# Softmax weights transposed by DMA, as two planes of two-byte words, instead of by TensorE

## The chip, the cores and the metric

The kernel runs on one core of a Trainium2 chip. The core has a matrix engine (TensorE, PE in the profile, with its weight loads as PEld), a vector engine (DVE), a scalar engine (ACT), GpSimd (POOL) and a queue engine that issues DMAs (SP). Each engine works through its own list of instructions in order; semaphores make one wait for another. The metric is the device time of one execution in microseconds (us), and less is better. Three runs of the kernel before took 2072.4, 2073.06 and 2074.07 us.

## The reference

Two transformer layers over 256 tokens of width 2048, all in float32. Each layer is a norm, an attention with 16 heads of 128, a residual, a norm, an MLP with squared ReLU (hidden 8192) and a residual; a last norm ends it. Layer 0 has 8 heads of neighbourhood attention and 8 of dilated attention, layer 1 has 16 heads over 4 shared key/value heads, with a sink logit per head. What matters here is the end of one head, cut down from the reference:

```python
s = jnp.einsum('nkgqd,nksd->nkgqs', qb, kb).astype(jnp.float32) * scale + bias
e = jnp.exp(s - m[..., None])
o = jnp.einsum('nkgqs,nksd->nkgqd', (e / den[..., None]).astype(v.dtype), vb)
```

The normalised weights `e / den` come out with queries along the partitions. The last product needs them with keys along the partitions, so each head's 256x256 weights are transposed once.

## The kernel before

Every large float32 operand is split into a high part that PE takes in its fast float32 form and a low rest (`split`, L92 to L94: ACT writes the high part, DVE the rest), and products of parts are summed. The weight matrices are streamed from DRAM in halves of 512 KB: `fetch` (L105) issues a load into a buffer `r` (six of them) on SP, ACT splits off `h` and DVE `l` (five buffers each), and PE uses them. `fetch` runs three halves ahead in the program; how far SP runs ahead on the chip is set by the `r` buffers.

A projection of one head is a `unit`: two halves, 16 matmuls with the low part (L154) and 16 with the high part (L156). Values for four heads, the output projection and the second MLP product go by `chunk` (L196), with the activations as the stationary operand. All of that is one stream of matmuls on PE. The attention of the heads is laid between these matmuls by a clock that the kernel keeps while it is built: `tick` advances it after each eight matmuls of a unit (four ticks a unit), and `later` puts a piece of work at a number of ticks ahead. Pieces marked narrow go only between the first halves of a unit unless they are four ticks late.

One head (`attend`) has three such pieces, with the distances in `LAGS_0`, `LAGS_1` and `LAGS_END`. `scores` (L341) multiplies q and k, adds the bias and takes the row minimum on DVE (L346), takes exponentials on ACT (L352), adds the sink in layer 1 (L350, L355, L356), and scales by the reciprocal sum on DVE (L359). `weights` (L362) transposes the weights on PE, four 128x128 blocks by a matmul against the identity (L366) into one PSUM buffer `p_ps`, and splits them into `pt`. `values` (L385) multiplies `pt` by the values `v`, and the result is split into `o`.

Layer 0 handles two heads at a time (four units a pair, and a value chunk at every other pair). Layer 1 has one unit of q per head, in two groups of eight heads with two units of k ahead of each. Its last heads' pieces fall into the output projection that follows. The queue of SP holds the weight loads of the whole program, a few loads at the start and the stores at the end, and nothing else. After the pieces are written down a scheduler settles the final order on each engine, moving work of the other engines around it; the order shown further down is the final one.

Of the kernel before, what the change touches and what calls it, by code (L numbers as in the profile page):

```python
# [7 lines left out]
F32 = mybir.dt.float32  # L8
# [6 lines left out]
P = 128  # L15
T = 256
# [14 lines left out]
RAW_BUFS = 6  # L31
PART_BUFS = 5

LAGS_0 = (5,4,3)
LAGS_1 = (4,5,3)
LAGS_END = (3,3,2)


def slopes(n):
# [4 lines left out]
def encoder(ctx: ExitStack, tc: tile.TileContext, a: dict, out: bass.AP):  # L44
    nc = tc.nc
# [7 lines left out]
    aux_ps = ctx.enter_context(tc.tile_pool(name="aux_ps", bufs=1, space=PSUM))  # L53
# [8 lines left out]
    ident = const.tile([P, P], F32, name="ident")  # L62
# [29 lines left out]
    def split(hi, lo, src):  # L92
        nc.scalar.activation(hi, src, AF.Copy)  # L93
        nc.vector.tensor_sub(lo, src, hi.bitcast(F32))  # L94
# [31 lines left out]
    def later(steps, fn, narrow=False):  # L126

        tasks.append((now[0] + steps, len(tasks), fn, narrow))
        tasks.sort(key=lambda t: t[0])
# [195 lines left out]
    def attend(pool, o, head, q, k, v, side, biases, lags, sunk=False):  # L325

        def scores():
            if not q or not k:

                state["late"] = True  # L330
                later(1, scores, True)
                return
            if state.pop("late", False):
                later(2 + 2 * (head % 2), scores, True)
                return
            qh, kh, bias = q[0], k[0], biases()
            s_ps = aux_ps.tile([P, 2, T], F32, name="s_ps", bufs=2)
            for i in range(2):
                qs = slice(i * P, (i + 1) * P)
                for n, (x, y) in enumerate(((0, 0), (0, 1), (1, 0))):  # L340
                    nc.tensor.matmul(s_ps[:, i, :], qh[:, x, qs], kh[:, y, :], start=n == 0, stop=n == 2)  # L341
            s = pool.tile([P, 2, T], F32, name="s", bufs=2)
            st = pool.tile([P, 8], F32, name="st", bufs=4)
            rd = pool.tile([P, 2], F32, name="rd", bufs=4)
            for i in range(2):
                nc.vector.tensor_tensor_reduce(s[:, i, :], s_ps[:, i, :], bias[i], -1.0, 3e38,  # L346
                                               ALU.add, ALU.min, st[:, i:i + 1])
            nm, den = st[:, 0:2], st[:, 2:4]
            if sunk:
                nc.vector.tensor_scalar(nm, nm, sink_neg[:, head:head + 1], None, op0=ALU.min)  # L350
            for i in range(2):
                nc.scalar.activation(s[:, i, :], s[:, i, :], AF.Exp, bias=st[:, i:i + 1], scale=-1.0,  # L352
                                     accum_out=st[:, 2 + i:3 + i])
            if sunk:
                nc.scalar.activation(st[:, 6:8], nm, AF.Exp, bias=sink[:, head:head + 1])  # L355
                nc.vector.tensor_add(den, den, st[:, 6:8])  # L356
            nc.vector.reciprocal(rd, den)
            for i in range(2):
                nc.vector.tensor_scalar(s[:, i, :], s[:, i, :], rd[:, i:i + 1], None, op0=ALU.mult)  # L359
            later(lags[1], lambda: weights(s), True)  # L360

        def weights(s):  # L362
            p_ps = aux_ps.tile([P, 2, T], F32, name="p_ps", bufs=1)
            for j in range(2):
                for i in range(2):
                    nc.tensor.transpose(p_ps[:, j, i * P:(i + 1) * P], s[:, i, j * P:(j + 1) * P], ident)  # L366
            pt = pool.tile([P, 2, 2, T], F32R, name="pt", bufs=2)
            split(pt[:, 0], pt[:, 1], p_ps)
            state["pt"] = pt
            state["at"] = now[0]  # L370
            try_values()

        def try_values():
            if not v or now[0] < state["at"] + lags[2]:
                later(1, try_values, True)
            else:
                values()

        def values():
            pt, vv = state["pt"], v[0]  # L380
            o_ps = aux_ps.tile([P, 512], F32, name="m_ps", bufs=2)
            n = 0
            for j in range(2):
                for x, y in ((0, 0), (0, 1), (1, 0)):
                    nc.tensor.matmul(o_ps[:, :T], vv[:, x, j, side * P:(side + 1) * P], pt[:, y, j, :],  # L385
                                     start=n == 0, stop=n == 5)
                    n += 1
            split(o[0][:, head, 0, :], o[0][:, head, 1, :], o_ps[:, :T])
            heads_done.add(head)

        state = {}
        later(lags[0], scores, True)
# [3 lines left out]
    def project_out(o, which):  # L396
        def done(c, ps, js):
            cs = slice(c * NC, (c + 1) * NC)
            for j in range(2):
                nc.vector.tensor_add(xs[:, j, cs], xs[:, j, cs], ps[j])  # L400
            to_features(c, which)
            for j in range(2):
                squares(c, j)

        def before():
            assert heads_done >= set(range(KT - 2))
            finish_tasks()
            assert heads_done == set(range(KT))

        for c in range(CHUNKS):  # L410
            chunk(o, KT, c, done, before if c == 0 else None)
            if c == 2:
                warm(AF.Sqrt, ssq[:, 0, 0:1])
        heads_done.clear()

    def toeplitz(pool, slope, which):
        def fn():

            if which == 1:
                t = pool.tile([P, 6, GRID], F32, name="rel", bufs=4).rearrange("p j c -> p (j c)")  # L420
            else:
                t = pool.tile([P, TW], F32, name="toep", bufs=2)
            nc.vector.scalar_tensor_tensor(t, tabs[:, 0, :], -slope, tabs[:, which, :],
                                           op0=ALU.mult, op1=ALU.add)
            return [t[:, P - P * i:P - P * i + T] for i in range(2)]
        return fn
# [147 lines left out]
    with tc.tile_pool(name="attn0", bufs=1) as pool:  # L574
# [14 lines left out]
        def grid_bias(h):  # L589
            def fn():  # L590
                rel = rels[h]
                return [rel[:, 2 - 2 * i:6 - 2 * i, :].rearrange("p j c -> p (j c)") for i in range(2)]
            return fn
# [29 lines left out]
        for p in range(8):  # L623
# [3 lines left out]
            for i in range(2):  # L627
                for j, (dst, name, sc) in enumerate(((q, "q", SCALE), (k, "k", 1.0))):
# [3 lines left out]
                    else:  # L632
                        unit(done)
                h = 2 * p + i
                attend(pool, o, h, q[i], k[i], v, h % 4,
                       grid_bias(h) if h < 8 else toeplitz(pool, sl[h - 8], 1), LAGS_0 if p < 7 else LAGS_END)
            if p < 3:
# [10 lines left out]
    with tc.tile_pool(name="attn1", bufs=1) as pool:  # L648
        o = [pool.tile([P, NH, 2, T], F32R, name="o")]
        sl = slopes(16)  # L650
        for p in range(2):
# [11 lines left out]
            for i in range(8):  # L663
# [3 lines left out]
                attend(pool, o, h, q, k[i // 4], v, h // 4, toeplitz(pool, sl[h], 2),  # L667
                       LAGS_1 if h < NH - 3 else LAGS_END, True)
        project_out(o[0], 3)
# [72 lines left out]
```

## Time and profile before

The profiled execution took 2072.76 us, of which 2071.0 us are the span from its first to its last instruction.

| | |
|---|---|
| median of 3 runs | 2073.06 us |
| profiled execution | 2072.76 us |
| span | 2071.0 us |
| granted clock of PE | 0.999 |
| DMA, mean | 187 GB/s |
| transposes on PE (L366) | 128, 19.4 us busy |
| values (L385) | 192, 27.7 us busy |
| scores (L341) | 192, 28.4 us busy |
| weight splits on ACT (L93, `h`) | 716, 757.6 us busy |
| weight splits on DVE (L94, `l`) | 716, 877.9 us busy |

The page gives busy time and its share of the span for each engine, then the chain of work that ended last: it is followed back from the last instruction, at each step to what released that instruction or to the one before it on the same engine. Matmuls are pipelined, so the busy time of a group (128 transposes of 273 ns, of which parts overlap) is more than the place that it takes in the chain; the chain in order of time gives the place. A row of a group of instructions has line, engine, operation, what it writes and reads, the count, then busy time and mean duration, then the engine's idle time just before.

### The profile page before, as it was taken

How to read it: one execution, taken by the hardware profiler on the slowest of the kernel's cores; microseconds unless marked ns; L12 is line 12 of the kernel's file. 1: busy time of each engine (PE TensorE's matmuls, PEld its weight loads, DVE VectorE, ACT ScalarE, POOL GpSimd, SP SyncE). 2: the span in 40 equal slices, each digit the busy share in tenths (PEclk: the TensorE clock that was granted, in tenths of full speed). 3: DMA queues.
4: the chain of work that ended last, by engine and by line, in shares of the span. 5: the costliest groups of instructions: out<-in, count | busy, mean ns of one | idle time of the engine just before them, and what ended most of it. 6: DMA issues, size and time to landing. Idle time of an engine off the chain costs nothing.

```text
span 2071.0 us, 27923 instructions
## 1 busy us (share of the span) xinstructions
PE 2059.9 (99%) x10714; PEld 1770.1 (85%) x10714; DVE 1267.7 (61%) x1790; ACT 1018.2 (49%) x1452; POOL 29.8 (1%) x43
## 2 busy tenths in 40 slices
PE   9999999999999999999999999999999999999998
PEld 8888888888888888888888998888888888888886
DVE  8767765666654456665546887566654446665454
ACT  7555555544533345454445666555443334554443
POOL 2200000000000000000000000000000000000000
PEclk9999999999999999999999999999999999999999
DMA  8755555555666655556655444565556665556663
GB/s 296 232 174 164 172 173 180 185 186 193 190 191 194 194 192 186 191 188 191 192 187 190 162 146 152 183 210 187 189 190 194 193 194 191 191 184 193 193 194 111
DMA packets 108164, 388.28 MB, mean 187 GB/s; under 512 B 12240, under 2 KB 13280, under 8 KB 107648
## 3 DMA queue, kind: packets, MB, share of 16 engines
q1 hardware_dynamic: 106128, 380.46, 57.1%
q0 software_dynamic: 1184, 4.74, 0.8%
q8 instruction: 84, 1.38, 0.3%
q10 hardware_dynamic: 720, 1.31, 0.2%
q14 instruction: 48, 0.39, 0.1%
HBM read 384.36 MB, written 2.10 MB: 187 GB/s over the span
## 4 chain that ended last, share of the span: by engine, by line
PE 98%; DVE 1%; ACT 0%; issue 0%; DVEq 0%
PE acc L156 31%; PE acc L196 26%; PE s_ps L196 21%; PE acc L154 16%; PE s_ps L341 1%; PE m_ps L385 1%; PE p_ps L366 1%; PE m_ps L241 1%; DVE l L94 0%; PE m_ps L518 0%; ACT h L93 0%; ACT gx L560 0%; PE p_ps L156 0%; PE s_ps L156 0%; DVE gx L562 0%
## 5 line engine op out<-in xcount | busy, mean ns | idle before, releaser
L94 DVE TENSOR_TENSOR l<-r,h 128x1024 fp32r<-128x1024 f32 (+1 forms) x724 | 883.5, 1220 | 477.7 <-ACT h L93 465.6
L93 ACT ACTIVATE h<-r 128x1024 fp32r<-128x1024 f32 (+1 forms) x724 | 762.6, 1054 | 538.3 <-PE acc L196 274.1
L156 PE MATMUL acc<-u,h 128*128 128x512 f32 x2848 | 685.8, 391 | 0.0
L156 PEld LDWEIGHTS acc<-u,h 128*128 128x128 f32 x2848 | 522.0, 188 | 99.9 <-ACT h L93 0.2
L154 PEld LDWEIGHTS acc<-u,l 128*128 128x128 f32 x2848 | 366.0, 191 | 12.5
L154 PE MATMUL acc<-u,l 128*128 128x256 f32 x2848 | 376.3, 283 | 0.0
L196 PE MATMUL s_ps<-h,hid 128*128 128x512 f32 x1024 | 317.0, 389 | 0.0
L196 PE MATMUL acc<-h,hid 128*128 128x512 f32 x1024 | 316.7, 389 | 0.0
L217 ACT ACTIVATE t<-acc 128x256 f32<-128x256 f32 x178 | 68.1, 383 | 428.3 <-PE acc L156 428.0
L219 DVE TENSOR_TENSOR z<-acc,t 128x256 f32<-128x256 f32 x178 | 75.7, 425 | 281.9 <-ACT t L217 281.9
L196 PEld LDWEIGHTS s_ps<-h,hid 128*128 128x128 f32 x1024 | 192.3, 188 | 39.7
L196 PEld LDWEIGHTS acc<-h,hid 128*128 128x128 f32 x1024 | 192.3, 188 | 39.7
L196 PE MATMUL s_ps<-l,hid 128*128 128x512 f32 x512 | 199.2, 389 | 0.0
L196 PE MATMUL acc<-l,hid 128*128 128x512 f32 x512 | 199.2, 389 | 0.0
L196 PEld LDWEIGHTS acc<-l,hid 128*128 128x128 f32 x512 | 96.1, 188 | 20.1
L196 PEld LDWEIGHTS s_ps<-l,hid 128*128 128x128 f32 x512 | 96.1, 188 | 19.9
L196 PE MATMUL acc<-h,u 128*128 128x512 f32 x288 | 94.9, 394 | 0.0
L196 PE MATMUL acc<-h,o 128*128 128x512 f32 x256 | 82.1, 392 | 0.0
L196 PE MATMUL s_ps<-h,o 128*128 128x512 f32 x256 | 80.6, 391 | 0.0
L196 PEld LDWEIGHTS acc<-h,u 128*128 128x128 f32 x288 | 54.1, 188 | 10.9
L439 DVE SCALAR_TENSOR_TENSOR z<-z 128x256 f32<-128x256 f32 x128 | 54.4, 425 | 4.3
L196 PEld LDWEIGHTS s_ps<-h,o 128*128 128x128 f32 x256 | 48.1, 188 | 9.9
(130 smaller groups left out, 1081.1 us busy)
## 6 DMA issues: line engine op xcount, KB each, us to landing
r<-in_w_mlp_in SPq DMA_DIRECT2D x256, 512.0 KB, 4.0
r<-in_w_mlp_out SPq DMA_DIRECT2D x256, 512.0 KB, 3.6
r<-in_even_w_in SPq DMA_DIRECT2D x56, 512.0 KB, 3.8
r<-in_odd_w_qkv SPq DMA_DIRECT2D x40, 512.0 KB, 3.8
r<-in_even_w_v SPq DMA_DIRECT2D x32, 512.0 KB, 4.3
r<-in_even_w_out SPq DMA_DIRECT2D x32, 512.0 KB, 3.5
r<-in_odd_w_out SPq DMA_DIRECT2D x32, 512.0 KB, 3.6
r<-in_odd_w_v SPq DMA_DIRECT2D x8, 512.0 KB, 3.5
```

The costliest lines, as they stand in the source:

```text
L93: nc.scalar.activation(hi, src, AF.Copy)
L94: nc.vector.tensor_sub(lo, src, hi.bitcast(F32))
L154: nc.tensor.matmul(ps[:, :T], l, u[:, k[n], 0, :], start=False, stop=stop)
L156: nc.tensor.matmul(ps, h, u[:, k[n]].rearrange("p a t -> p (a t)"), start=k[n] == 0, stop=stop)
L196: nc.tensor.matmul(ps[j], act[:, k, x, tokens], y, start=k == 0 and n == 0, stop=k == nk - 1 and n == 2)
L217: nc.scalar.activation(t, ps[:, T:], AF.Copy)
L219: nc.vector.tensor_add(z, ps[:, :T], t)
L241: nc.tensor.transpose(ps[k // 2][:, k % 2, j * P:(j + 1) * P], xs[:, j, (k0 + k) * P:(k0 + k + 1) * P], ident)
L341: nc.tensor.matmul(s_ps[:, i, :], qh[:, x, qs], kh[:, y, :], start=n == 0, stop=n == 2)
L366: nc.tensor.transpose(p_ps[:, j, i * P:(i + 1) * P], s[:, i, j * P:(j + 1) * P], ident)
L385: nc.tensor.matmul(o_ps[:, :T], vv[:, x, j, side * P:(side + 1) * P], pt[:, y, j, :], start=n == 0, stop=n == 5)
L439: nc.vector.scalar_tensor_tensor(z, z, 0.0, z, op0=ALU.max, op1=ALU.mult)
```

## The change

The four transposes on PE go. In their place `weights` treats each float32 weight as two 16-bit words. Two ACT copies (L369) gather the low words and the high words of all weights into two planes (`planes`). Each plane is transposed as four 128x128 blocks of two-byte words by transposing DMAs on SP (L372), eight a head, into `turned`. A new piece, `join`, set at a fourth distance after `weights`, writes the words back into place: ACT the low words (L379) and DVE the high words (L380) of `pw`, which is then split into `pt` as `p_ps` was. `planes`, `turned` and `pw` have one buffer each. The distances in ticks are changed too.

```diff
-LAGS_0 = (5,4,3)
-LAGS_1 = (4,5,3)
-LAGS_END = (3,3,2)
+LAGS_0 = (5,4,2,5)
+LAGS_1 = (4,4,2,5)
+LAGS_END = (3,3,1,4)
...
         def weights(s):
-            p_ps = aux_ps.tile([P, 2, T], F32, name="p_ps", bufs=1)
-            for j in range(2):
-                for i in range(2):
-                    nc.tensor.transpose(p_ps[:, j, i * P:(i + 1) * P], s[:, i, j * P:(j + 1) * P], ident)
+
+            half = mybir.dt.uint16
+            words = s.rearrange("p i t -> p (i t)").bitcast(half).rearrange("p (i t w) -> p w i t", i=2, w=2)
+            planes = pool.tile([P, 2, 2, T], half, name="planes", bufs=1)
+            turned = pool.tile([P, 2, 2, T], half, name="turned", bufs=1)
+            for w in range(2):
+                nc.scalar.copy(planes[:, w], words[:, w])
+                for j in range(2):
+                    for i in range(2):
+                        nc.sync.dma_start(turned[:, w, j, i * P:(i + 1) * P], planes[:, w, i, j * P:(j + 1) * P],
+                                          transpose=True)
+            later(lags[3], lambda: join(turned), True)
+
+        def join(turned):
+            p = pool.tile([P, 2, T], F32, name="pw", bufs=1)
+            words = p.rearrange("p j t -> p (j t)").bitcast(mybir.dt.uint16).rearrange("p (j t w) -> p w j t", j=2, w=2)
+            nc.scalar.copy(words[:, 0], turned[:, 0])
+            nc.vector.tensor_copy(words[:, 1], turned[:, 1])
             pt = pool.tile([P, 2, 2, T], F32R, name="pt", bufs=2)
-            split(pt[:, 0], pt[:, 1], p_ps)
+            split(pt[:, 0], pt[:, 1], p)
```

In the new file lines after `weights` have moved by 14: values are L399. On SP, in layer 1 after the loads of the first units, before (with -) and now (with +), the transposes stand in line with the weight loads `r`:

```order
 L109 DMA r<-in_odd_w_v 128x1024 x8
-L109 DMA r<-in_odd_w_qkv 128x1024 x36
-L109 DMA r<-in_odd_w_out 128x1024 x32
+L109 DMA r<-in_odd_w_qkv 128x1024 x16
+L372 DMA_TRANSPOSE turned<-planes 128x128 x8
+L109 DMA r<-in_odd_w_qkv 128x1024 x2
+L372 DMA_TRANSPOSE turned<-planes 128x128 x8
+L109 DMA r<-in_odd_w_qkv 128x1024 x2
+L372 DMA_TRANSPOSE turned<-planes 128x128 x4
+L109 DMA r<-in_odd_w_qkv 128x1024
+L372 DMA_TRANSPOSE turned<-planes 128x128 x4
```

Between two heads' eight transposes stand two loads, the two halves of one unit. On ACT, in the same layer, one head before took these rows (`t` and `h` belong to the stream of projections, `s` is the exponential, `o` the result of an earlier head):

```order
L93 ACTIVATE pt<-p_ps 128x512
L352 ACTIVATE s,st<-s,st 128x256 x2
L355 ACTIVATE st<-st,sink 128x2
L217 ACTIVATE t<-acc 128x256
L93 ACTIVATE h<-r 128x1024
L93 ACTIVATE q<-z 128x256
L93 ACTIVATE h<-r 128x1024
L93 ACTIVATE o<-m_ps 128x256
```

Now, from one head's `pw` to the next head's `planes`:

```order
L379 COPY pw<-turned 128x512
L352 ACTIVATE s,st<-s,st 128x256 x2
L355 ACTIVATE st<-st,sink 128x2
L217 ACTIVATE t<-acc 128x256
L93 ACTIVATE pt<-pw 128x512
L93 ACTIVATE h<-r 128x1024
L93 ACTIVATE q<-z 128x256
L93 ACTIVATE o<-m_ps 128x256
L369 COPY planes<-s 128x512 x2
L93 ACTIVATE h<-r 128x1024
```

The next head's `planes` stand behind this head's `pw` and `pt`, and three copies have been added. On PE, in the middle of layer 1's first group of heads, before (-) and now (+), where L385 and L399 are the values:

```order
-L154 MATMUL acc<-u,l 128x256 x8
-L366 MATMUL p_ps<-ident,s 128x128 x4
-L154 MATMUL acc<-u,l 128x256 x8
-L156 MATMUL acc<-u,h 128x512 x16
-L385 MATMUL m_ps<-pt,v 128x256 x6
+L154 MATMUL acc<-u,l 128x256 x16
+L156 MATMUL acc<-u,h 128x512 x16
+L399 MATMUL m_ps<-pt,v 128x256 x6
 L341 MATMUL s_ps<-k,q 128x256 x6
```

The transposes are gone from the stream. The values of a head now stand three units behind its scores, where they stood two behind before: the first values of layer 1 come after the third head's scores.

## The prediction

> **What bounds the kernel now.** I read the page's first part, then the chain that ended last, then that chain in order of time where the softmax weights are transposed, and last what ACT and DVE have left there.
>
> ```profile
> span 2071.0 us, 27923 instructions
> PE 2059.9 (99%) x10714; PEld 1770.1 (85%) x10714; DVE 1267.7 (61%) x1790; ACT 1018.2 (49%) x1452; POOL 29.8 (1%) x43
> PE 98%; DVE 1%; ACT 0%; issue 0%; DVEq 0%
> ```
>
> PE is the bound: it is never idle and it is 98% of the chain. So each matmul taken off it is worth its place in the chain, as long as nothing new makes PE wait. The chain in order of time, in layer 1's attention (start, length, piece):
>
> ```profile
> 1177.14 0.71 PE m_ps L385 x6
> 1177.86 0.72 PE s_ps L341 x6
> 1178.58 0.96 PE acc L154 x8
> 1179.54 0.44 PE p_ps L366 x4
> 1179.97 0.96 PE acc L154 x8
> 1180.93 3.65 PE acc L156 x16
> 1184.59 0.71 PE m_ps L385 x6
> ```
>
> One head takes 7.44 us from values to values (1177.14 to 1184.59): a unit (0.96 + 0.96 + 3.65 = 5.57), scores 0.71, values 0.71 and the four transposes 0.44. The table of stages, over exactly two such heads, shows what is left on the other engines (columns: stage, its length, then busy time of PE, PEld, DVE, ACT, POOL):
>
> ```profile
> 1187.51:1202.39 14.88, 14.88 (x99) 13.59 (x98) 13.52 (x35) 9.87 (x22) 0.00 (x0) 1.00 0.43 141
> ```
>
> Per head DVE works 6.76 of 7.44 us and ACT 4.94. The slack is on ACT; DVE has 0.7 us.
>
> **Removed.** 32 heads x 0.44 us = 14.1 us of PE. A layer-1 head then needs 5.57 + 0.71 + 0.71 = 7.0 us of PE. The old reader of `p_ps`, the split into `pt`, stays and reads `pw`.
>
> **Added, per head.** Two ACT copies into `planes`, eight transposing DMAs on SP, one ACT copy and one DVE copy into `pw`. The nearest rows, 128 partitions by 512 elements:
>
> ```profile
> L93 ACT ACTIVATE pt<-p_ps 128x512 fp32r<-128x512 f32 x32 | 19.0, 592 | 17.9 <-PE p_ps L366 17.7
> L94 DVE TENSOR_TENSOR pt<-p_ps,pt 128x512 fp32r<-128x512 f32 x32 | 21.9, 685 | 0.2
> ```
>
> I take 0.59 us for a copy on ACT and 0.69 on DVE; half of each, and a fifth more, bound them, which moves the sum by a few us. ACT then has 4.94 + 3 x 0.59 = 6.7 us of work in 7.0, DVE 6.76 + 0.69 = 7.45 in 7.0. Already without any wait DVE is over by 0.45 us a head.
>
> The trace of before has no transposing DMA. The rows nearest to it are the plain ones: the issue of a weight load on SP, the dearest issue (POOL's `rev`), and the landing of `rev`, which at 54.8 KB is nearest in size to 32 KB.
>
> ```profile
> L109 SPq DMA_DIRECT2D r<-in_odd_w_qkv x40: 327/328/328, 1077.3 to 1223.0; - x40
> L605 POOL DMA_DIRECT2D rev<-in_rpb x16: 522/526/591, 29.9 to 83.4; - x16
> DMA to landing us min/median/max: 2.4/3.6/13.2
> ```
>
> Call T the time from the first issue of a head's eight to the last landing. Low: 7 x 0.33 + 2.4 = 4.7 us. Chosen: 7 x 0.53 + 3.6 = 7.3 us, since a transposing DMA is no simpler than the dearest plain one and lands among weight loads, as the median of `rev` did. High: each lands before the next begins, 8 x 2.4 = 19.2 us. Below 4.7 it would have to land sooner than any DMA of this trace; that is a rival.
>
> SP issues the transposes in line with the weight loads, so a waiting transpose holds up the loads behind it. That is covered: a load is issued six `r` buffers ahead, with two halves a head 6 x 3.5 = 21 us before its split, and lands in 3.8 us, so 17 us are spare:
>
> ```profile
> r<-in_odd_w_qkv SPq DMA_DIRECT2D x40, 512.0 KB, 3.8
> ```
>
> A price for the issue is stated by the Trainium skill, "VectorE: DVE Perf Modes", section "The three transpose paths": 1309 ns for one 128x128 two-byte transpose by DMA, against 390 by TensorE. No run here shows the first; for the second the chain has 0.44 / 4 = 0.11 us. With 1.309 as issue time, an estimate from that page, T = 7 x 1.309 + 3.6 = 12.8 and the sum below comes to about +200 us, 2270. Against that, the Trainium skill, "Advanced Engine Details and Errata", section "X-Bar Transpose (TRN2)", says that such transposes are as fast as regular DMAs. By it the issue is the 0.33 us of the weight loads, T = 5.9, and the same sum gives +36 us, 2109. Neither is shown by a run here.
>
> **What the transposes collide with.** `planes`, `turned` and `pw` have one buffer each. The eight transposes of head h+1 cannot start before both copies of head h into `pw` are done, and ACT and DVE run in order. From the last landing of h to the first issue of h+1 stand, by the order of ACT: the DVE copy 0.69 (the `pt` split waits for it), `pt` 0.59, an `h` split 1.05, `planes` 0.59, and in half of the heads also `q` and `o`. Rows for these:
>
> ```profile
> 1190.59 1.05 ACT L93 ACTIVATE h<-r 128x1024 fp32r<-128x1024 f32 x1
> 1191.71 0.42 ACT L93 ACTIVATE q<-z 128x256 fp32r<-128x256 f32 x1
> 1193.03 0.36 ACT L93 ACTIVATE o<-m_ps 128x256 fp32r<-128x256 f32 x1
> ```
>
> 0.69 + 0.59 + 1.05 + 0.59 + 0.39 = 3.3 us (0.39 is half of `q` and `o`). So layer 1 has a cycle C = T + 3.3 = 10.6 us a head, against 7.0 of PE. **The wait that takes the place of the transposes is PE's L399, values, on the DVE half of `pt`.**
>
> How much of it is hidden? From the first score of a head to its scaled weights:
>
> ```profile
> 1185.13 0.88 PE L341 MATMUL s_ps<-k,q 128*128 128x256 f32 x6
> 1190.13 0.62 DVE L359 TENSOR_SCALAR s<-s,rd 128x256 f32<-128x256 f32 x2
> ```
>
> 5.62 us (1190.75 - 1185.13). Then `h` 1.05, `planes` 0.59, T, the DVE copy 0.69, `pt` 0.59 + 0.69: 9.2 + T = 16.5 us. In the new order the first values stand three units and three score blocks behind their scores, 3 x (5.57 + 0.71) = 18.8 us: a margin of 2.3.
>
> Layer 1 comes in two groups of eight heads. Between the values of the first and the last head of group one, PE has 7 units, 7 value and 5 score blocks, 47.5 us; it waits 7 x 10.6 - 47.5 - 2.3 = 24.4 us. In group two the last values lie inside the output projection: 2 2/3 units, 7 value and 5 score blocks and 66 matmuls of 0.227 (43.52 / 192, from the chain's row below), 38.5 us; it waits 74.2 - 38.5 - 2.3 = 33.4 us. Layer 1: 57.8 us.
>
> ```profile
> 616.55 43.52 PE s_ps L196 x192
> ```
>
> Layer 0 has 16 heads in 279 us, 17 us each, so the cycle doesn't bind. The stages, layer 1's attention first:
>
> ```profile
> 1145.00:1280.00 135.00, 135.00 (x841) 121.53 (x840) 114.30 (x279) 84.28 (x183) 0.00 (x0) 1.00 0.46 149
> 31.00:310.00 279.00, 278.00 (x1550) 241.75 (x1550) 199.05 (x354) 152.98 (x256) 21.06 (x29) 1.00 0.58 186
> ```
>  But at three of the value chunks (pairs 2, 4 and 6) ACT has only `planes`, `h` and `pw` (2.23 us) between the issue and a `pt` that waits for all eight transposes, and the chunk's `v` copies, on which values wait, are queued behind: 3 x (7.3 + 0.69 - 2.23) = 17.3 us. By PE's new order, at the chain's paces, the last two heads have 13.4 and 12.4 us from scores to values for a chain that without the sink (0.6 us less) takes 15.9: 3.5 us, the first wait carrying over to the second. Layer 0: 20.8 us. Its other heads have some 18 us and are covered; if T passes 9 they are not.
>
> **Sum.** -14.1 + 57.8 + 20.8 = +64.5 us on the profiled execution's 2072.76 us (span 2071.0 and 1.8 around it): 2137 us. The median of the three runs, 2073.06, is 0.3 above that execution, which is nothing here.
>
> **The rivals.** (A) The forecast's mechanism with T between 4.7 and 9: at 4.7, C = 8.0, waits 3.6 + 12.6 + 9.4 + 0.9, sum +12, 2085; at 9, C = 12.3, waits 38.0 + 47.0 + 22.3 + 5.2, sum +98, 2171. Chance 50%.
>
> (B) Dear transposes: one instruction is worked off as a chain of small moves, or each waits for the one before, T from 9 to 19.2. At 12: C = 15.3, the margin is gone (-2.4), waits 62.0 + 71.0 in layer 1, 31.4 + 8.3 and up to 8 x 2.3 for heads no longer covered in layer 0, sum +177, 2250. At 19.2 it is +378, 2451, and the 17 us that cover the weight loads are gone too. For it: eight dependent landings lie on one queue. Against: plain DMAs of one queue overlap. The twelve first loads were issued within 11 us, each 0.4 us long, and landed 4.4 us after their issue:
>
> ```profile
> L530 SPq DMA_DIRECT2D gx<-in_gx x12: 328/427/635, 0.7 to 11.4; - x12
> DMA to landing us min/median/max: 3.3/4.4/7.1
> ```
>
> Chance 34%.
>
> (C) Faster: a copy inside the chip lands sooner than any load here. At T = 4.0 C is 7.3, the waits are 7 in group two and 7.3 at the chunks, and the sum is zero; that is the point from which it decides. At T = 3 only 4.4 us are left at the chunks, the sum is -10 us, and DVE, 0.45 us over per head, takes some of it through later `l` splits: about 2065 us. For it: the trace has only DMAs that read or write DRAM, so nothing shows the landing of this one. Against: eight issues alone take 2.6 us at the cheapest. Chance 10%.
>
> (D) No change: T between the two, 3.7 to 4.3, gains and waits cancel; 2073 us. Chance 6%. That the transposes aren't made is excluded by the order, which has 256 of them and no L366.
>
> **How the numbers follow.** The predicted time is that of A at its chosen T, 2137 us. A and D lie between 2069 and 2171. B adds the upper side; I stop at 2330 (T near 15), which leaves out about 8 in 100 above, and at 2069 below, which leaves out C. About 0.2% (4 us) is what a measurement of this kernel can tell from no change. Faster 10%, within it 6%, slower 84%.
>
> **What would show it.** Right: rows of L372 with an issue of some 0.5 us and 3 to 4 us to landing; PE idle before L399, released by DVE `pt`, some 50 to 60 us in layer 1; ACT idle before `pw`, released by a DMA on `turned`; layer 1's attention, 135 us long before (1145 to 1280), at some 185; no L366. The MLPs unchanged. The size is wrong if T per head isn't 7 us; the mechanism is wrong if PE waits for weight splits instead (SP starved), or if heads of layer 1 follow at 7.5 us with ACT and DVE always busy (C).

## The result and the profile after

The change takes 2292.23 us (median of four, 2289.92 to 2293.43) against 2073.22 for the kernel before on the same chip: a ratio of 1.105 with an interval of 1.104 to 1.107, 219 us slower. The prediction had the sign and the kind of wait, and less than a third of the size. The page of the changed kernel (span, busy time by engine, the granted clock in 40 slices of 57 us, the chain by engine):

```profile
span 2290.1 us, 28206 instructions
...
PE 2115.5 (92%) x10586; PEld 1802.8 (79%) x10586; DVE 1270.1 (55%) x1822; ACT 1066.1 (47%) x1548; POOL 26.7 (1%) x43
...
PEclk9989898999999999999999878799999999999999
...
PE 75%; SPq 11%; DVE 5%; DMA 4%; ACT 3%; issue 1%; DVEq 0%; ACTq 0%
```

PE was idle for 11.1 us of the span before (2071.0 - 2059.9) and is for 174.6 now: 163.5 more. Its busy time should have fallen by the 14.1 us of the transposes, to 2045.8, and is 69.7 above that. 163.5 + 69.7 - 14.1 = 219.1 us, the whole loss. The clock digits fall where the two attentions lie, and nowhere else.

Where each layer loses is read from the start of the first 43.52 us block of each MLP, in the chain in order of time; before:

```profile
573.03 43.52 PE acc L196 x192
...
1535.70 43.52 PE acc L196 x192
```

and after:

```profile
676.84 43.52 PE acc L196 x192
...
1755.36 43.52 PE acc L196 x192
```

Layer 0's attention has become 103.8 us longer, layer 1's 115.9 (219.7 - 103.8); the MLPs take what they took. What the transposes cost on SP (minimum, median and maximum in ns, then the landing) and who stands for them (total us, times, longest), from the view of one line and from the view of waits:

```profile
L372 SPq DMA_TRANSPOSE turned<-planes x256: 1093/1230/2527, 49.7 to 1493.6; - x128
...
DMA to landing us min/median/max: 2.2/2.4/10.3
```

```profile
DVE pw L380 <- DMA turned<-planes: 250.8, 32, 9.2
ACT pw L379 <- DMA turned<-planes: 114.1, 27, 8.6
...
PE m_ps L399 <- ACT pt L93: 69.8, 17, 6.7
...
PE m_ps L399 <- ACT v L319: 31.8, 3, 10.6
...
PE acc L196 <- DVE z L219: 18.9, 4, 6.6
```

SP stands 1.23 us at each transposing DMA, not 0.53, and one lands 2.4 us after its issue begins, not 3.6. The chain through one head of layer 1 shows the eight one after the other (start, length, piece):

```profile
1258.98 0.52 ACT planes L369
...
1259.56 1.11 SPq L372
...
1260.72 1.22 SPq L372
...
1268.36 2.41 DMA turned<-planes
...
1270.90 0.47 DVE pw L380
...
1273.60 1.13 ACT planes L369 x2
```

From 1259.5 to the last landing at 1270.8 are T = 11.3 us, and from one head's `planes` to the next 14.6 us (1273.60 - 1258.98), against 7.0 of PE's work. Over the seven steps of each group of eight heads the mean from first issue to first issue is 14.4 and 14.3 us. In layer 1's attention PE is busy for two thirds, at a clock of 0.81, and in layer 0's for 81%, at 0.90 (same columns as the stages before):

```profile
31.00:414.00 383.00, 308.54 (x1525) 260.53 (x1523) 203.61 (x371) 177.56 (x305) 20.48 (x28) 0.90 0.48 147
1249.00:1500.00 251.00, 165.59 (x784) 140.72 (x783) 116.39 (x296) 109.80 (x232) 0.00 (x0) 0.81 0.33 99
```

### The profile page after: what moved, and what is told of

The parts are those of the page before. It is cut to its first block, busy times and chain, and to the rows that moved or that the text cites. A ratio compares the mean times of both kernels' runs of the same rounds, so it can differ in the third digit from the quotient of the medians.

```text
span 2290.1 us, 28206 instructions
## 1 busy us (share of the span) xinstructions
PE 2115.5 (92%) x10586; PEld 1802.8 (79%) x10586; DVE 1270.1 (55%) x1822; ACT 1066.1 (47%) x1548; POOL 26.7 (1%) x43
## 4 chain that ended last, share of the span: by engine, by line
PE 75%; SPq 11%; DVE 5%; DMA 4%; ACT 3%; issue 1%; DVEq 0%; ACTq 0%
PE acc L156 23%; PE s_ps L196 19%; PE acc L196 19%; PE acc L154 12%; SPq L372 11%; DMA turned<-planes 3%; DVE l L94 2%; ACT planes L369 1%; ACT h L93 1%; DVE pw L380 1%; PE m_ps L399 1%; DVE s L359 1%; PE m_ps L241 0%; DVE pt L94 0%; DVE s L346 0%
## 5 line engine op out<-in xcount | busy, mean ns | idle before, releaser
L156 PE MATMUL acc<-u,h 128*128 128x512 f32 x2848 | 686.4, 391 | 0.1
L156 PEld LDWEIGHTS acc<-u,h 128*128 128x128 f32 x2848 | 522.9, 189 | 100.1 <-ACT h L93 0.3
L154 PEld LDWEIGHTS acc<-u,l 128*128 128x128 f32 x2848 | 383.2, 200 | 12.6
L154 PE MATMUL acc<-u,l 128*128 128x256 f32 x2848 | 389.4, 291 | 0.0
L399 PE MATMUL m_ps<-pt,v 128*128 128x256 f32 x192 | 53.5, 420 | 119.8 <-ACT pt L93 69.8
L380 DVE COPY pw<-turned 128x512 uint16<-128x512 uint16 x32 | 14.6, 456 | 250.8 <-DMA turned<-planes 250.8
L399 PEld LDWEIGHTS m_ps<-pt,v 128*128 128x128 f32 x192 | 41.2, 290 | 136.1 <-ACT pt L93 78.5
L196 PE MATMUL acc<-h,o 128*128 128x512 f32 x256 | 88.1, 417 | 6.6 <-DVE z L219 6.6
L379 ACT COPY pw<-turned 128x512 uint16<-128x512 uint16 x32 | 24.7, 772 | 128.3 <-DMA turned<-planes 114.1
```

What stands on the lines that cost most here:

```text
L154: nc.tensor.matmul(ps[:, :T], l, u[:, k[n], 0, :], start=False, stop=stop)
L156: nc.tensor.matmul(ps, h, u[:, k[n]].rearrange("p a t -> p (a t)"), start=k[n] == 0, stop=stop)
L196: nc.tensor.matmul(ps[j], act[:, k, x, tokens], y, start=k == 0 and n == 0, stop=k == nk - 1 and n == 2)
L379: nc.scalar.copy(words[:, 0], turned[:, 0])
L380: nc.vector.tensor_copy(words[:, 1], turned[:, 1])
```

## The experiments

"MLPs at" gives the start of the first 43.52 us block of layer 0's MLP (573.03 before) and of layer 1's (1535.70 before). Each diff is against the change, that of e12 against the kernel before; `...` stands for lines left out.

**e1, the distances alone.** The weights are transposed by PE as before, but with the change's distances, at the place of `join`:

```diff
-        def join(turned):
+        def join(s):
+            p = aux_ps.tile([P, 2, T], F32, name="p_ps", bufs=1)
+            for j in range(2):
+                for i in range(2):
+                    nc.tensor.transpose(p[:, j, i * P:(i + 1) * P], s[:, i, j * P:(j + 1) * P], ident)
```

> The new distances and the place of the join stay, but at the join the four transposes go by TensorE again; no planes, no DMAs, no copies into pw. Theory S (the serial issue of eight transposing DMAs on SP, 1.23 us each in the trace, makes T = 11 us and so the cycle): the kernel is back at 2073 us, within 8. Rival W (the new distances, that is the later values and the other order, cost by themselves): most of the +219 us stays, over 2180.

2074.01 us against 2073.49, ratio 1.0002 (0.9992 to 1.0011). The new distances and the new order on PE cost nothing.

**e2, the copies alone.** No DMAs; `join` copies from `planes`.

```diff
-                for j in range(2):
-                    for i in range(2):
-                        nc.sync.dma_start(turned[:, w, j, i * P:(i + 1) * P], planes[:, w, i, j * P:(j + 1) * P],
-                                          transpose=True)
-            later(lags[3], lambda: join(turned), True)
+            later(lags[3], lambda: join(planes), True)
```

> Left out: the eight transposes; the join copies the planes back as they are, so the weights are multiplied untransposed. All three ACT copies and the DVE copy stay. Theory S: 14 us of TensorE are saved and only some microseconds of crowding on DVE come back, 2058 to 2066. Rival A (the added copies on ACT and DVE fill these engines): DVE at 7.2 us of work per head in 7.0 alone would give 2062 to 2070, and if it were the cause of the loss, over 2150.

2058.46 us, ratio 0.9926 (0.9911 to 0.9941): 15 us are gained, and layer 0's MLP starts at 566.03. PE's 14.1 us are really on the path, and 96 more copies on ACT and 32 more on DVE are nearly free, even in layer 1 where DVE seemed over by 0.45 us a head.

**e3, half of the DMAs.** Only the high words are transposed by DMA, four a head; the low words go into `pw` as they are.

```diff
-                for j in range(2):
-                    for i in range(2):
-                        nc.sync.dma_start(turned[:, w, j, i * P:(i + 1) * P], planes[:, w, i, j * P:(j + 1) * P],
-                                          transpose=True)
+            for j in range(2):
+                for i in range(2):
+                    nc.sync.dma_start(turned[:, j, i * P:(i + 1) * P], planes[:, 1, i, j * P:(j + 1) * P],
+                                      transpose=True)
...
-            nc.scalar.copy(words[:, 0], turned[:, 0])
+            nc.scalar.copy(words[:, 0], planes[:, 0])
```

> Left out: the transposes of the low words, which are joined untransposed; four DMAs per head in place of eight. Theory S: T = 3 x 1.23 + 2.4 = 6.1 us, cycle 9.4 us by the prediction's sum, waits 14.8 + 23.8 in layer 1 and some 16 in layer 0, less 14: about 2113, and down to 2065 since ACT waits for no transposed plane. Rival Q (the traffic of the transposes delays the weight loads): half the traffic, half the loss, about 2180.

2153.1 us, ratio 1.038 (1.037 to 1.040), between the two. The issue stays 1.23 us, so T is about 6.2. MLPs at 611.15 and 1615.88:

```profile
611.15 43.52 PE acc L196 x192
...
1615.88 43.52 PE acc L196 x192
```

Layer 1 loses 42 us, where the sum of the prediction with T = 6.2 gives 33; layer 0 loses 38, where it gives 9. So the sum lacks something, most of it in layer 0.

**e4, layer 1 alone.** Layer 0 by PE with its old distances.

```diff
+            if not by_dma:
+                p_ps = aux_ps.tile([P, 2, T], F32, name="p_ps", bufs=1)
...
+        by_dma = sunk
...
```

> Layer 0 goes by TensorE with the old distances, layer 1 by DMA with the new ones. Between the starts of the same MLP matmuls layer 0's part grew by 103.8 us and layer 1's by 115.9 us. If the two are apart, 2073 + 116 = 2189 us. If the loss in layer 1 comes from something that layer 0 leaves behind (a clock that stays low, a queue that is late), under 2160.

2189.6 us, ratio 1.056 (1.054 to 1.058), 116 us more than before: what layer 1 loses in the whole change. The two layers' losses are apart and add up.

**e5, two large DMAs a head.** The same bytes, one DMA of 128x512 words a plane; `planes` are laid out so that the four blocks follow each other.

```diff
...
-                for j in range(2):
-                    for i in range(2):
-                        nc.sync.dma_start(turned[:, w, j, i * P:(i + 1) * P], planes[:, w, i, j * P:(j + 1) * P],
-                                          transpose=True)
...
+                nc.sync.dma_start(turned[:, w].rearrange("p j t -> p (j t)").rearrange("p (g c) -> p g c", g=4),
+                                  planes[:, w].rearrange("p j i c -> p (j i c)"), transpose=True)
```

> One transposing DMA for each plane, 128x512 words, in place of four of 128x128: two a head instead of eight, the same bytes. Theory I (SP is held 1.23 us for each instruction, whatever its size): T = 1.23 + 2.4 = 3.6 us, C = 3.6 + 3.3 = 6.9, below the 7.0 us of PE, so nearly no waits and about 2060 to 2075 us; the rows of L372 still show 1.2 us. Rival B (SP is held by the amount of data): each row shows about 4 x 1.23 = 4.9 us, T stays 11 to 12, and the time stays within 20 us of the change's 2292.

2067.04 us, ratio 0.9968 (0.9956 to 0.9979): faster than the kernel before. The line's view and the page's PE row:

```profile
L371 SPq DMA_TRANSPOSE turned<-planes x64: 1200/1210/1786, 49.3 to 1271.0; - x64
...
DMA to landing us min/median/max: 2.4/2.6/6.2
```

```profile
PE 2049.4 (99%) x10586; PEld 1757.4 (85%) x10586; DVE 1272.7 (62%) x1822; ACT 1066.1 (52%) x1548; POOL 26.8 (1%) x43
```

Four times the data for the same 1.21 us: SP is held for each instruction, not for its bytes. T is now 1.2 + 2.6 = 3.8 us. With as many bytes transposed by DMA as in the change, PE is within 4 us of the 2045.8: the bytes slow no matmul.

**e6, all 256 issued, nobody waits.** `join` copies from `planes`, which have two buffers; `turned` is written and not read.

```diff
-            planes = pool.tile([P, 2, 2, T], half, name="planes", bufs=1)
+            planes = pool.tile([P, 2, 2, T], half, name="planes", bufs=2)
...
-            later(lags[3], lambda: join(turned), True)
+            later(lags[3], lambda: join(planes), True)
```

> All 256 transposing DMAs are issued as in the change, but nobody reads what they write: the join copies from the planes (the weights stay untransposed, this part is left out), and the planes have two buffers. Theory S (the price is the wait of the join, in ACT's and DVE's order, for eight issues one after the other): layer 0 loses nothing, its first 43.52 us MLP block comes at or before 573; in layer 1 SP has 8 x 1.27 + 2 x 0.33 = 10.8 us of issues a head against 7.0 of PE, so the weight loads fall behind by 3.8 us a head from the point where their lead of some 17 us is used up: 10 to 45 us there. In all 2065 to 2110 us. Rival R (the transposes cost by their traffic or by what they do to other loads, not by the wait): layer 0 is late as well, over 2150 us in all.

2127.02 us, ratio 1.026 (1.024 to 1.027). The first matmul of layer 0's MLP product starts at 573.17, before at 572.87, so layer 0 is no later than before although SP issues all its transposes; that speaks against rival R. But in e2, without the DMAs, layer 0's MLP comes 7 us sooner (566.03): the DMAs take back what the missing transposes give there. Layer 1 is 53 us longer, above the 45 expected, and the largest wait is not the one expected. Weight loads do come late, and ACT waits for them, 26.3 us in layer 0 and 18.2 us in layer 1; but longer than that in layer 1 ACT stands at `planes` until an earlier head's transposes have read them:

```profile
ACT planes L369 <- DMA turned<-planes: 44.5, 9, 9.9
...
ACT h L93 <- DMA r<-in_even_w_in: 23.1, 7, 10.1
...
ACT h L93 <- DMA r<-in_odd_w_qkv: 12.8, 2, 8.3
```

So SP's issues by themselves (8 x 1.27 = 10.2 us a head against 7.0 of PE) bind layer 1 even if nobody reads what they write.

**e7, fillers in PE's waits.**

```diff
+            if sunk:
+                spare = aux_ps.tile([P, 512], F32, name="p_ps", bufs=1)
+                for _ in range(16):
+                    nc.tensor.matmul(spare, u[:, 0, 0, :P], u[:, 0].rearrange("p a t -> p (a t)"), start=True, stop=True)
             o_ps = aux_ps.tile([P, 512], F32, name="m_ps", bufs=2)
```

> The change, with 16 matmuls of 128x512 that nobody reads put on PE ahead of each head's values in layer 1, 16 x 0.227 = 3.6 us, where PE now waits 65.7 us over 16 heads (4.1 each). Theory K (about 70 us of the loss are matmuls at a lower granted clock, which falls because PE waits; 43 of them in layer 1): the fillers lie in the waits, the granted clock of layer 1's stretch (0.75 to 0.84) comes back above 0.95, and the time falls by 20 to 40 us, to 2250 to 2272. Rival N (the matmuls there are slower for another reason, such as the transposes' traffic): the clock rows and the matmuls stay as they are, and the time stays at 2292 or grows by up to 20 us where a filler is longer than the wait.

2315.39 us, 23 more than the change: a miss, and it decides nothing. PE's idle time ahead of scores and values in layer 1 fell only from 79 to 53 us for 58 us of fillers, so they lay partly on the path, and the waits that were left (up to 13.9 us) still lowered the clock there. e12 asks the question again, the other way round.

**e8, a longer distance in layer 0.** DMAs for heads 0 to 13 of layer 0 alone, ten steps to `join`, two buffers each.

```diff
-LAGS_0 = (5,4,2,5)
+LAGS_0 = (5,4,2,10)
...
-            planes = pool.tile([P, 2, 2, T], half, name="planes", bufs=1)
-            turned = pool.tile([P, 2, 2, T], half, name="turned", bufs=1)
+            planes = pool.tile([P, 2, 2, T], half, name="planes", bufs=2)
+            turned = pool.tile([P, 2, 2, T], half, name="turned", bufs=2)
...
```

> Transposes by DMA only for heads 0 to 13 of layer 0, joined ten steps after their issue instead of five, with two buffers of planes and of turned; heads 14 and 15 and layer 1 by TensorE with the distances of before. Theory S (only the wait costs): 13 us from planes to the landing lie within ten steps of about 1.4 us, no wait is left, and 14 x 0.44 = 6.2 us of PE are gained: 2067 us, ratio 0.997. Rival (the transposes cost in layer 0 beside the wait, by ACT's and DVE's order or by the loads behind them on SP): 2075 us or more.

2159.14 us, ratio 1.041 (1.040 to 1.043): 85 us lost where 6 were to be gained. ACT in order of time shows why (start, length, line, and in brackets the idle time before it with its releaser):

```profile
211.00 0.61 ACT L376 COPY planes<-s 128x512 uint16<-128x512 uint16 x1
211.51 1.05 ACT L94 ACTIVATE h<-r 128x1024 fp32r<-128x1024 f32 x1
212.47 0.40 ACT L94 ACTIVATE k<-z 128x256 fp32r<-128x256 f32 x1
212.77 1.04 ACT L94 ACTIVATE h<-r 128x1024 fp32r<-128x1024 f32 x1
217.01 0.76 ACT L386 COPY pw<-turned 128x512 uint16<-128x512 uint16 x1 [3.19 <-DMA turned<-planes]
222.92 0.63 ACT L94 ACTIVATE pt<-pw 128x512 fp32r<-128x512 f32 x1 [5.15 <-DVE pw L387]
```

The ten steps moved nothing on ACT: behind `planes` still stand two `h` and one `k`, 2.5 us of work, and then this head's `pw`, which needs transposes that SP has only begun. In the change the same copy, at 218.52 us, stands behind two `h`, one `k` and one `o`. The scheduler that settles each engine's order has put the copy there. ACT stands 3.2 + 5.2 us, and `t`, `q` and the next `h` are queued behind.

**e9, layer 0's join on GpSimd.** The eight DMAs stay; in layer 0 GpSimd makes both copies and the split.

```diff
-LAGS_0 = (5,4,2,5)
+LAGS_0 = (5,4,5,10)
...
+            else:
+                for w in range(2):
+                    nc.gpsimd.tensor_copy(words[:, w], turned[:, w])
+                nc.gpsimd.tensor_copy(pt[:, 0], p)
+                nc.gpsimd.tensor_tensor(pt[:, 1], p, pt[:, 0].bitcast(F32), op=ALU.subtract)
```

> The change, but in layer 0 GpSimd makes both copies into pw and the split into pt (and the values stand eight PE steps later), so that neither ACT nor DVE stands at a transposing DMA there; the eight DMAs a head stay as they are. Theory O (layer 0 loses its 104 us because ACT and DVE run in order: the copies into pw stand some 3 us of ACT's work behind planes, both engines stand there for 8 us a head, and the v, z, k and l that PE needs are queued behind them): layer 0 loses at most 10 us, its first 43.52 us MLP block starts at 566 to 583, layer 1 stays 116 us late, and the whole takes 2175 to 2200 us. Rival P (it is PE's own wait for the late weights, whoever joins them): the first MLP block stays at 640 or later, and the whole above 2250 us.

2201.64 us, ratio 1.062 (1.060 to 1.063). MLPs at 585.43 and 1664.28:

```profile
585.43 43.52 PE acc L196 x192
...
1664.28 43.52 PE acc L196 x192
```

Layer 0's loss falls from 103.8 to 12.4 us, a little over the 10 expected, and layer 1 keeps its 116. GpSimd now stands at the transposes, but the `v`, `z`, `k` and `l` that PE needs are not queued behind it:

```profile
POOL pw L386 <- DMA turned<-planes: 193.9, 30, 25.9
```

Two things changed at once here: GpSimd makes the join, and the distances are longer. e8 has the longer distance to the join and gains nothing by it; the later values alone were not run. Waits are left in layer 0: PE's, 10.9 us for the `pt` that GpSimd makes, and ACT's, 29.8 us at `planes` for transposes and 22.9 us for weight loads, which stand in SP's line with the transposes.

**e10, one DMA a head.** 128x1024 words, both planes.

`planes` are laid out as in e5, and the one call stands behind both copies.

```diff
...
+            nc.sync.dma_start(turned.rearrange("p w j t -> p (w j t)").rearrange("p (g c) -> p g c", g=8),
+                              planes.rearrange("p w j i c -> p (w j i c)"), transpose=True)
```

> One transposing DMA a head, 128x1024 words, both planes. Theory I (SP is held about 1.2 us an instruction): the row of L370 stays at 1.2 to 1.3 us, T is 1.2 + 2.6 = 3.8 us but starts only after the second copy into planes, as late as with two DMAs: 2064 to 2069 us. Rival B' (held by the instruction up to some size, by the data beyond it): the row shows 2.4 us or more, the landing is later by as much, and the time is 2070 us or more.

2064.9 us, ratio 0.9958 (0.9944 to 0.9972), 9 us less than before and the fastest kernel here that makes the transposes. Eight times the data still holds SP for 1.24 us; only the landing grows:

```profile
L371 SPq DMA_TRANSPOSE turned<-planes x32: 1237/1238/1991, 50.0 to 1268.9; - x32
...
DMA to landing us min/median/max: 3.0/3.8/6.6
```

The landing is counted from the start of the issue, so T is 3.8 us, as with two DMAs.

**e11, two DMAs, both copies into `pw` on GpSimd.** The DMAs are those of e5; `planes` and `turned` have two buffers.

```diff
...
-            nc.scalar.copy(words[:, 0], turned[:, 0])
-            nc.vector.tensor_copy(words[:, 1], turned[:, 1])
+            for w in range(2):
+                nc.gpsimd.tensor_copy(words[:, w], turned[:, w])
```

> Two DMAs a head of 128x512 words, two buffers of planes and of turned, and both copies into pw made by GpSimd, which is 1% busy, instead of by ACT and DVE. Of the 14.1 us that PE no longer works, two DMAs a head alone gave back 7 (PE 2049.4 busy where 2045.8 is the least, 4.8 more idle). If what they give back is DVE's and ACT's time at the two copies (0.46 and 0.77 us a head and the waits in front of them): 2059 to 2064 us. Rival: GpSimd's copies are slower than 3 us each, pt comes later than the values, and the time is 2070 us or more.

2082.71 us, ratio 1.004 (1.003 to 1.006), 16 us worse than e5. Neither expectation holds: a copy takes GpSimd 0.78 us, not 3, yet the time is in the rival's range. The split of `pt` still stands in ACT's order, and ACT waits 81.0 us (29 times) for GpSimd in front of it. Here, moving a part of the join off ACT and DVE saved nothing while another part kept its place there. e5 has one buffer each of `planes` and `turned`; what the second ones do was not run alone.

**e12, waits without DMAs.** The kernel before, with ACT delayed in layer 1:

```diff
+            if sunk:
+                idle = pool.tile([P, 2, T], F32, name="idle", bufs=1)
+                for _ in range(12):
+                    nc.scalar.activation(idle, p_ps, AF.Copy)
             pt = pool.tile([P, 2, 2, T], F32R, name="pt", bufs=2)
```

> The kernel before, without any transposing DMA; in layer 1 ACT copies p_ps twelve times into a tile that nobody reads, ahead of the split into pt: 12 x 0.6 = 7.2 us a head, so ACT has 4.94 + 7.2 = 12.1 us of work against 7.44 of PE, and PE waits some 4 to 5 us a head, 16 times. Theory K (the granted clock falls because PE waits, whatever it waits for): PE's busy time grows from 2059.9 by 0.4 to 0.55 us for each us of its idle time, the granted clock of layer 1's stretch falls to 0.75 to 0.9, and the span is 2071 plus both. Rival N (the slow matmuls belong to the transposing DMAs): PE's busy time stays at 2060, the clock at 0.99, and the span grows by the idle time alone.

2133.93 us, ratio 1.029 (1.028 to 1.031). The page's PE row, two stretches of 40 us before and during the waits, and two waits, the first and the longest, with the six value matmuls behind each, which take 0.88 us in the same view of the kernel before:

```profile
PE 2082.8 (98%) x10714; PEld 1781.9 (84%) x10714; DVE 1269.2 (60%) x1790; ACT 1113.6 (52%) x1644; POOL 27.9 (1%) x43
```

```profile
1220.00:1260.00 40.00, 40.00 (x235) 34.48 (x234) 30.97 (x63) 37.64 (x76) 0.00 (x0) 1.00 0.54 168
1260.00:1300.00 40.00, 23.13 (x89) 18.65 (x87) 16.47 (x47) 31.16 (x69) 0.00 (x0) 0.74 0.18 53
```

```profile
1267.63 2.16 PE L389 MATMUL m_ps<-pt,v 128*128 128x256 f32 x6 [2.53 <-ACT pt L93]
...
1292.54 2.16 PE L389 MATMUL m_ps<-pt,v 128*128 128x256 f32 x6 [6.54 <-ACT pt L93]
```

PE waits for `pt` eight times only, all after 1260 us. It has 48.2 us of idle time, 37.1 more than before, and is busy for 22.9 us more with the same 10714 matmuls: 0.62 us a us, a little more than expected, and no transposing DMA in the kernel. Theory K stands: the granted clock falls right after PE's waits also where no transposing DMA is in the kernel. The Trainium skill, "TensorE: Matmul & The Clock Gate", section "Part 1: The HAM clock gate (the "warmup" mystery)", says that the clock goes to half after an idle window of some 3.4 us. The half agrees with the trace: from 1267.6 to 1273 us, right behind the first wait, the granted clock is 0.50. The length does not: that wait is 2.53 us, and the matmuls behind it are as slow as those behind the wait of 6.54.

## Why the prediction was half right

The forecast was +64.5 us; +219 were measured. The cycle of layer 1 was the right mechanism with one wrong term, T; in layer 0 the step that calls most heads covered was wrong.

- **Each matmul off PE is worth its place: right.** e2 gains 15 us for the 14.1 counted.
- **The copies cost little: right.** The added copies take 0.61 us (`planes`) and 0.77 (`pw`) on ACT and 0.46 on DVE, near the 0.59 and 0.69 taken.
- **T, 7 x 0.53 + 3.6 = 7.3 us: the term that was mis-sized.** The issue of a transposing DMA was set by the dearest plain one; it is 1.23 us, 2.3 times that, and the eight go one after the other. With the 0.04 us between two of them T is 7 x 1.27 + 2.4 = 11.3 us. e5 and e10 show that this is a price for each instruction. That put the kernel into rival B, whose chance was 34 in 100: not for slow landings, which are faster than those of the loads, but for the issue. The Trainium skill, "VectorE: DVE Perf Modes", section "The three transpose paths", has 1309 ns for such a transpose, near the 1230 of the trace, without saying that this is the issue, as the prediction assumed in its estimate of 2270. The rule of the Trainium skill in "Advanced Engine Details and Errata", section "X-Bar Transpose (TRN2)", that they are as fast as regular DMAs doesn't hold for SP's issue (1.23 us against 0.33 for a load of 512 KB).
- **The return path of 3.3 us, the cycle and the margin in layer 1: right.** With T = 11.3 the sum of the prediction has C = 14.6, near the 14.3 to 14.4 measured, and the margin becomes -1.7 (18.8 - 9.2 - 11.3): waits of 7 x 14.6 - 47.5 + 1.7 = 56.4 and 102.2 - 38.5 + 1.7 = 65.4, together 121.8, less 7.0 of PE: 114.8 us. Measured: 115.9 in the change, 116 in e4. The way from a landing to the next issue is as predicted in some heads; in others, as in the chain above, it goes through DVE's `toep`, `z` and `s`, which the sum left out, and takes about as long, so that the 3.3 us fits them is in part luck. PE's idle time in front of the values in layer 1 is mostly put down to ACT's half of `pt` (53.6 us), not DVE's (11.5) as forecast; the two halves follow each other.
- **Layer 0, "Its other heads have some 18 us and are covered": the step that failed.** With T = 11.3 the value chunks give 3 x (11.3 + 0.69 - 2.23) = 29.3 us, and the trace has 31.8 there on ACT's half of `v`, three times; the last two heads give 7.5. That is 30 us of loss after the gain of 7.0, and 43 with the 8 x 1.6 us that rival B's term for heads no longer covered gives at this T, against 103.8 measured. The prediction said itself that these heads aren't covered when T passes 9, but priced that at 1.6 us a head for half of them. The prediction asked how long PE has between a head's scores and its values. What decides is how much work ACT and DVE have between `planes` and `pw` in their own order: one `k` and two `h`, 2.5 us, where T is 11. So both stand at every head, and PE waits later, for `z`, `k`, `l` and `v` that were queued behind. e8 shows the place, e6 that the DMAs without the wait cost layer 0 no more than its gain of 7 us, and e9 that the loss goes to 12 us when another engine stands there and the values come later.
- **SP holds no weight load back: right for the change.** In the whole trace PE is idle for 0.1 us in front of the matmuls that read new weights in units (L154, L156), and ACT waits 0.4 us for a load. It isn't right by itself: where ACT and DVE don't stand at the join, loads come late (e6, e9).
- **The clock was not in the sum.** PE's busy time has 69.7 us too much, in stretches with a lower granted clock. This isn't a further 70 us on top of the mechanism everywhere: layer 1 comes out at 116 without it, as its cycle is set by SP, ACT and DVE, and slower matmuls there fill time in which PE would have waited. So PE is idle for 85.4 us in that stage (251.00 - 165.59) where the sum has 121.8 of waits. How much the lower clock adds to layer 0's loss, no run tells apart.
- **The signs named beforehand.** The MLPs are unchanged, ACT stands in front of `pw`; but L372 shows 1.23 us and not 0.5, and layer 1's attention takes 251 us, not 185. PE's idle time before the values in layer 1 is 65.7 us, near the 50 to 60 named; that is luck, since the sum with the measured T has 121.8 there and slower matmuls and other waits take up the rest.

## What to carry to other kernels

Count the DMAs of a step as a chain on the queue that issues them, and before dropping the idea, make them fewer and larger: one transposing DMA a head instead of eight turned 219 us lost into 9 gained. When an engine is to read what a DMA brings, look at how much work stands in that engine's own order between the source and the read, since the distance in the program's steps need not survive the scheduler. And where PE sets the time, price a wait of PE above its length, since the matmuls behind it run slower.

## What was not expected of the hardware

A transposing DMA inside the chip held SP for 1.23, 1.21 and 1.24 us at 128, 512 and 1024 columns of two-byte words on 128 partitions, and landed 2.4, 2.6 and 3.8 us after the start of the issue. With no transposing DMA in the kernel, waits of PE of 2.5 to 6.5 us brought its granted clock to 0.50 right behind them and to 0.74 over 40 us, and each us of added idle time came with 0.62 us of added busy time.
